# Two blocks' gate and up projections of the last feed-forward part as a two by two block product in seven products

## The chip, the cores and the metric

The kernel runs on one core of one Trainium2 chip. The metric is the device time of one execution in microseconds (us), as the median of several runs. The profile beside it is of one execution.

## The reference, cut to what matters

A two-layer decoder trunk over 256 tokens of width 1024. Each layer is a feed-forward part, a mixer and a second feed-forward part, so four feed-forward parts run in all: (layer 0, 1), (0, 2), (1, 1) and (1, 2). The change is in the last of them, (1, 2).

```python
def rms_norm(x, gain):
    y = x * rsqrt(mean(x * x, axis=-1) + 1e-6)
    return y * gain

def swiglu(h, w_gate, w_up, w_down):          # h 256x1024, w_gate and w_up 1024x2816, w_down 2816x1024
    return (silu(h @ w_gate) * (h @ w_up)) @ w_down

for layer in range(2):
    x = x + 0.5 * swiglu(rms_norm(x, ffn1_norm[layer]), ...)
    x = x + mixer(layer, x)                   # layer 0: mLSTM, layer 1: dilated attention
    x = x + 0.5 * swiglu(rms_norm(x, ffn2_norm[layer]), ...)   # layer 1: part (1, 2)
```

All arrays are float32.

## The kernel before, in words

**Three products for one.** A float32 operand is split into two parts of the type fp32r, `hi` (the rounded value) and `lo` (what is left). `mm3` then issues three matmuls for one product: `xh·wl`, `xh·wh`, `xl·wh`, each with 128 rows and up to 512 columns. Every weight therefore passes through a split: ScalarE writes `hi`, VectorE subtracts and writes `lo`.

**Tiles of a feed-forward part.** The 2816 hidden columns are 11 blocks of 256 (b = 0 to 10). For a block, the gate and the up columns stand side by side, 512 columns in all, in one PSUM bank. The 256 tokens are two halves t of 128. `gu(b, t)` is 8 steps k of 128 rows, 24 matmuls. The weights of one block are four units of two k each ([128, 1024] float32, 512 KB); each unit is used twice, by t = 0 and by t = 1. `dn(b, t)` multiplies the hidden values by the block's two units of `w_down` into PSUM accumulators: 12 matmuls for each t. Between them lies the activation: ScalarE `sil`, VectorE `h`, VectorE transposes into `hb`, which goes to DRAM (`hd`) and comes back turned (`ht`), and is split into `hhb` and `hlb` (`hidden_blocks`, `placed`).

**Order.** The matmuls' order is written out in `ffn_in`: `gu(0)`, `gu(1)`, then `gu(b)` followed by `dn(b - 2)`. `_stream` lists the weight units in the same order. A planner with a cost model (`_Model`) runs while the program is built; it places the work of ScalarE, VectorE and the queues between the matmuls by the time at which it expects operands, and so fixes the order of instructions on each engine. An engine takes its instructions in that order and waits for whichever is first.

**Rings.** `RAW` = 6 raw units may be loaded or in work. `RING` = 9 pairs of `hi` and `lo` tiles hold split units; unit n can be split when unit n - 9 has been used for the last time. Loads go out on SP's queue; no DMA is issued from POOL.

**Gains.** The norm's gain can be multiplied into x (`transposed` with a gain: four ScalarE and four VectorE instructions of 128 columns for four chunks) or into the weights (`FOLDED`: the split of one unit is then two ScalarE and two VectorE instructions of 512 columns, with a gain for each k). Part (1, 2) has its gain in the weights, and `mixer_b` ends with `then(None)`.

```python
    def loads(self):
        while self.loaded < len(self.units) and len(self.raw) + len(self.running) < RAW and \
                (self.units[self.loaded][1] is not None or self.loaded == self.next):
            self.load_unit()
```

Of the kernel before, what the change touches and what calls it, by code (L numbers as in the profile page):

```python
# [28 lines left out]

RING = 9  # L30
RAW = 6
# [19 lines left out]

FOLDED = {("kv",): 3, ("gu", 1, 1): 4, ("bq",): 5, ("gu", 1, 2): 6, ("mkv", 0): 7, ("mkv", 1): 8}

# [4 lines left out]
def folded(key):  # L58

    return next((FOLDED[key[:n]] for n in (1, 2, 3) if key[:n] in FOLDED), None)  # L60


def _stream():
# [26 lines left out]
    def ffn(layer, which):  # L90
        g, u, d = (f"ffn{which}_w_{s}" for s in ("gate", "up", "down"))

        def gu(b):
            lo, hi = b * FB, (b + 1) * FB
            proj(("gu", layer, which, b), None, layer, ((g, lo, hi), (u, lo, hi)), 2)

        def dn(b):
            for c in range(2):
                rows = "turned" if turned(layer, which, b) else None
                units.append((("dn", layer, which, b, c), (d, layer, rows, 2 * b + c, 1), D))  # L100

        gu(0)
        for b in range(1, NB - 1):
            gu(b)
            if (layer, which, b) in MEMORY:
                memory(MEMORY[layer, which, b])
            if b > 1:
                dn(b - 2)
            if b in AHEAD_OF.get((layer, which), ()):
                c = next(order)  # L110
                units.append((("pre", c), ("b_w_out", 0, None, c, 1), D))
        gu(NB - 1)
        for b in range(NB - 3, NB):
            dn(b)
# [12 lines left out]
    for b in range(2):  # L127
        single(("bq", b), "b_w_q", 0, b * 512, (b + 1) * 512, 2)
    for c in B_ORDER:
        units.append((("bo", c), None, D))  # L130
    ffn(1, 2)
    return units


def _pack(units, w):

    parts = []
    for _, src, _ in units:
        if src is None:
# [147 lines left out]
class _Engine:  # L287
# [5 lines left out]
    def __getattr__(self, method):  # L293
        call, model, name = getattr(self.engine, method), self.model, self.name

        def traced(out, *args, **kw):
# [4 lines left out]
            n = out.free_size()  # L301
            if method == "dma_start" and name != "sync":
                model.run(name, 1.0 if name == "gpsimd" else 0.1, outs, ins, 2.5)
                return
            if name == "sync":
                model.run(name, max(n * out.partition_size() * 4 / 360e3, 0.06), outs, ins, 2.0)
                return
# [50 lines left out]
class _Kernel:  # L358
    def __init__(self, tc, ctx, io, out, units):
# [3 lines left out]
        self.units = units  # L363
        self.index = {u[0]: i for i, u in enumerate(units)}
        self.offset = []
        off = 0
        for _, src, width in units:
            self.offset.append(off)
            off += P * width if src else 0
        self.tiles = {}  # L370
# [5 lines left out]
        self.raw = {}  # L376
        self.stored = {}
        self.side = []
# [122 lines left out]
    def load_unit(self):  # L501
        i, self.loaded = self.loaded, self.loaded + 1
        if self.units[i][1] is None:
            return
        width = self.units[i][2]
        raw = self.rawp.tile([P, 1024], F32, tag="raw", name=f"raw{i}")
# [4 lines left out]
        self.raw[i] = raw  # L511

    def parts(self, i):
# [4 lines left out]
    def emit_unit(self):  # L518
# [12 lines left out]
        def steps(raw):  # L531
            if key[0] == "memT" and folded(("mkv", key[1])) is None:
                raw3 = raw.rearrange("p (k t) -> p k t", k=4)
                gain = self.gains[7 + key[1]][:, 4 * key[2]:4 * key[2] + 4]
                self.nc.gpsimd.tensor_tensor(
                    raw3, raw3, gain.unsqueeze(2).to_broadcast([P, 4, 2 * P]), ALU.mult)
                yield
            gain, k, each = folded(key), src[3], width // src[4]
            if gain is None:
# [4 lines left out]
            else:  # L544
# [8 lines left out]
            self.running.remove(c)  # L553
            self.loads()
# [15 lines left out]
        c = self.spawn(steps(self.raw.pop(i)))  # L570
        self.running.append(c)
        self.step(c)
# [4 lines left out]
    def loads(self):  # L577

        while self.loaded < len(self.units) and len(self.raw) + len(self.running) < RAW and \
                (self.units[self.loaded][1] is not None or self.loaded == self.next):  # L580
            self.load_unit()

    def room(self):
        while len(self.raw) + len(self.running) >= RAW:
            self.finish(self.running[0])

    def unit_ready(self):
# [8 lines left out]
        if i not in self.raw:  # L596
            return 1e9
        at = max(model.ready(self.raw[i][:, :self.units[i][2]]),
                 model.free((id(self.ring), "hi"), RING), model.free((id(self.ring), "lo"), RING))
# [13 lines left out]
    def release(self, *key):  # L613
        i = self.index[key]
        self.used[i] += 1
        while self.freed < len(self.units) and \
                self.used[self.freed] == (1 if self.units[self.freed][0][0] in ("memT", "pre") else 2):
            self.tiles.pop(self.freed)
            self.freed += 1

    def matmul(self, out, lhsT, rhs, start, stop):
        self.pe.matmul(out, lhsT=lhsT, rhs=rhs, start=start, stop=stop)  # L624
        n = out.free_size()
# [7 lines left out]

    def mm3(self, ps, x, w, start, stop):
        (xh, xl), (wh, wl) = x, w
        self.matmul(ps, xh, wl, start, False)
        self.matmul(ps, xh, wh, False, False)
        self.matmul(ps, xl, wh, False, stop)
        self.tick()
# [207 lines left out]
    def ffn(self, layer, which, after, memory=None):  # L847
        with ExitStack() as ctx:
            self.ffn_in(layer, which, after, memory, self.pool(ctx, f"ffn{layer}{which}"))

    def ffn_in(self, layer, which, after, memory, fp):
# [4 lines left out]
        nc = self.nc  # L856
        acc, chains, hT, blocks, made = [], {}, {}, {}, {}

        def activated(ps, t, out, last=False):
# [25 lines left out]
        def hidden_blocks(b, t):  # L885
            def steps(ps):
                h = self.work.tile([P, FB], F32, tag="ta", bufs=4, name="h")
                yield from activated(ps, t, h)
                if b not in blocks:
                    blocks[b] = fp.tile([P, 4, 2, 2, 32], F32, tag="hb", bufs=1, name="hb")  # L890
                nc.vector.transpose(blocks[b][:, :, :, t, :].rearrange("p j c t -> p c j t"),
# [68 lines left out]

        for b in range(NB - 1):
            if (layer, which, b) == (0, 1, 0):
# [4 lines left out]
                continue  # L967
            if (layer, which, b) == (0, 1, 1):
# [4 lines left out]
            else:  # L973
                for t in range(2):
                    gu(b, t)
            if (layer, which, b) in MEMORY:
                memory()
            if 1 < b < NB - 1:
                for t in range(2):
                    dn(b - 2, t)  # L980
        gu(NB - 1, 0)
        dn(NB - 3, 0)
        gu(NB - 1, 1)
        dn(NB - 2, 0)
        dn(NB - 1, 0)
        for b in range(NB - 3, NB):
            dn(b, 1)
# [594 lines left out]
    def run(self, stop=None):  # L1582
# [58 lines left out]
        if stop == 2:  # L1641
            return
        with ExitStack() as ctx:
            self.shared = self.pool(ctx, "shared")
            self.ffn(0, 2, store if stop == 3 else then(None))
            if stop == 3:
                return
# [55 lines left out]
```

## Time and profile before

| | |
|---|---|
| median of 3 runs | 988.46 us (987.95 to 988.94) |
| the profiled execution's own time | 988.44 us |
| span from its first to its last instruction | 986.7 us |
| TensorE (PE) busy | 979.1 us, 99% of the span, 4679 matmuls |
| VectorE (DVE) busy | 641.8 us, 65% |
| ScalarE (ACT) busy | 569.6 us, 58% |
| granted TensorE clock | 1.000 |

The time lies 1.74 us above the span. The last feed-forward part takes the span from about 803 us to the end. A matmul's row gives its own latency (about 0.39 us for 512 columns); matmuls overlap, and their rate is read from how many start in a stretch.

### The profile page before, as it was taken

How to read it: one execution, taken by the hardware profiler on the slowest of the kernel's cores; microseconds unless marked ns; L12 is line 12 of the kernel's file. 1: busy time of each engine (PE TensorE's matmuls, PEld its weight loads, DVE VectorE, ACT ScalarE, POOL GpSimd, SP SyncE). 2: the span in 40 equal slices, each digit the busy share in tenths (PEclk: the TensorE clock that was granted, in tenths of full speed). 3: DMA queues.
4: the chain of work that ended last, by engine and by line, in shares of the span. 5: the costliest groups of instructions: out<-in, count | busy, mean ns of one | idle time of the engine just before them, and what ended most of it. 6: DMA issues, size and time to landing. Idle time of an engine off the chain costs nothing.

```text
span 986.7 us, 13121 instructions
## 1 busy us (share of the span) xinstructions
PE 979.1 (99%) x4679; PEld 813.3 (82%) x4679; DVE 641.8 (65%) x988; ACT 569.6 (58%) x914; POOL 43.1 (4%) x78
## 2 busy tenths in 40 slices
PE   9999999999999999999999999999999999999998
PEld 6887888899998888888888888888887788888887
DVE  6856656567868766575576676676566776675752
ACT  7656545478786645455476565565564585454540
POOL 0001000010010000000012000000002000000000
PEclk9999999999999999999999999999999999999999
DMA  9967777346436588878657687789537457767641
GB/s 365 329 211 273 245 229 225 107 158 202 160 129 235 190 301 265 290 269 273 219 179 252 212 304 239 250 307 325 181 106 262 187 172 245 247 206 247 206 149 43
DMA packets 84905, 221.84 MB, mean 225 GB/s; under 512 B 8108, under 2 KB 29544, under 8 KB 84840
## 3 DMA queue, kind: packets, MB, share of 16 engines
q1 hardware_dynamic: 84696, 220.97, 66.7%
q8 instruction: 36, 0.59, 0.2%
q14 instruction: 29, 0.24, 0.1%
q10 hardware_dynamic: 144, 0.04, 0.0%
HBM read 201.56 MB, written 19.42 MB: 224 GB/s over the span
## 4 chain that ended last, share of the span: by engine, by line
PE 85%; ACT 2%; DVE 2%; issue 1%; POOL 1%; ACTq 0%; DVEq 0%
PE gups L624 43%; PE acc L624 23%; PE aps L624 5%; PE oacc L624 4%; PE kvps L624 3%; PE bqps L624 2%; PE mkvps L624 1%; PE tps L631 1%; ACT L297 1%; DVE lo L297 1%; DVE s L297 1%; PE tpp L631 1%; PE po L624 1%; ACT mp L297 0%; PE ms L624 0%
## 5 line engine op out<-in xcount | busy, mean ns | idle before, releaser
L297 DVE TENSOR_TENSOR lo<-raw,hi 128x1024 fp32r<-128x1024 f32 (+3 forms) x235 | 267.9, 1161 | 75.9 <-ACT hi L297 69.9
L297 ACT CAST hi<-raw 128x1024 fp32r<-128x1024 f32 (+3 forms) x235 | 230.8, 1003 | 88.1 <-PE acc L624 37.2
L624 PE MATMUL gups<-lo,xh 128*128 128x512 f32 x704 | 273.4, 390 | 0.0
L624 PE MATMUL gups<-hi,xh 128*128 128x512 f32 x704 | 272.7, 389 | 0.1
L624 PE MATMUL gups<-hi,xl 128*128 128x512 f32 x704 | 272.7, 389 | 0.0
L297 DVE SCALAR_TENSOR_TENSOR lo<-raw,gains,hi 128x512 fp32r<-128x512 f32 x232 | 160.9, 745 | 34.5 <-ACT hi L297 31.9
L297 ACT ACTIVATE hi<-raw,gains 128x512 fp32r<-128x512 f32 x232 | 153.2, 716 | 46.3 <-PE acc L624 22.5
L624 PEld LDWEIGHTS gups<-hi,xh 128*128 128x128 f32 x704 | 132.1, 188 | 27.8 <-ACT hi L297 0.8
L624 PEld LDWEIGHTS gups<-hi,xl 128*128 128x128 f32 x704 | 132.2, 188 | 27.5
L624 PEld LDWEIGHTS gups<-lo,xh 128*128 128x128 f32 x704 | 132.2, 188 | 27.4 <-DVE lo L297 0.2
L297 ACT ACTIVATE sil<-gups,rstd 128x256 f32<-128x256 f32 x88 | 41.5, 473 | 162.1 <-PE gups L624 159.5
L297 DVE SCALAR_TENSOR_TENSOR h<-gups,rstd,sil 128x256 f32<-128x256 f32 x88 | 42.1, 480 | 127.7 <-ACT sil L297 127.7
L624 PE MATMUL acc<-lo,hhb 128*128 128x512 f32 x304 | 119.5, 393 | 0.0
L624 PE MATMUL acc<-hi,hlb 128*128 128x512 f32 x304 | 118.4, 390 | 0.0
L624 PE MATMUL acc<-hi,hhb 128*128 128x512 f32 x304 | 118.3, 389 | 0.0
L624 PEld LDWEIGHTS acc<-hi,hlb 128*128 128x128 f32 x304 | 57.1, 188 | 11.9
L624 PEld LDWEIGHTS acc<-hi,hhb 128*128 128x128 f32 x304 | 57.1, 188 | 11.4
L624 PEld LDWEIGHTS acc<-lo,hhb 128*128 128x128 f32 x304 | 57.1, 188 | 11.4
L624 PE MATMUL aps<-lo,xh 128*128 128x384 f32 (+1 forms) x144 | 49.6, 345 | 0.7 <-ACT sg L297 0.7
L624 PE MATMUL aps<-hi,xl 128*128 128x384 f32 (+1 forms) x144 | 47.5, 330 | 0.0
L624 PE MATMUL aps<-hi,xh 128*128 128x384 f32 (+1 forms) x144 | 47.4, 329 | 0.0
L297 DVE STREAM_TRANSPOSE hb<-h 128x256 f32<-128x256 f32 x76 | 33.6, 442 | 15.5 <-DMA hd<-hb 14.2
(194 smaller groups left out, 990.6 us busy)
## 6 DMA issues: line engine op xcount, KB each, us to landing
raw<-in_wts SPq DMA_DIRECT2D x310, 512.0 KB, 4.7
raw<-in_wts SPq DMA_DIRECT2D x32, 384.0 KB, 3.8
hd<-hb SPq DMA_DIRECT2D x38, 256.0 KB, 5.3
ht<-hd SPq DMA_DIRECT2D x38, 256.0 KB, 4.5
wo<-hi SPq DMA_DIRECT2D x8, 512.0 KB, 6.7
wo<-lo SPq DMA_DIRECT2D x8, 512.0 KB, 6.7
hi<-wo SPq DMA_DIRECT2D x8, 512.0 KB, 4.7
lo<-wo SPq DMA_DIRECT2D x8, 512.0 KB, 6.6
```

The lines of the kernel that those rows point to most:

```text
L297: call(out, *args, **kw)
L624: self.pe.matmul(out, lhsT=lhsT, rhs=rhs, start=start, stop=stop)
L631: self.pe.transpose(out, in_, ident)
```

## The change

The weights of blocks 5 and 6 of part (1, 2), `[1024 rows, 512 + 512 columns]`, are seen as a two by two matrix: two halves of the 1024 rows by the two blocks. x is two by two as well: two token halves by two halves of the 1024 columns. Instead of eight products of 128 tokens x 512 x 512 columns, seven are made (numbered 1 to 7 in `SEVEN`), of sums and differences of the parts of x and of the weights, and the four results are put together from the seven.

- `PLANS` gives the order of part (1, 2): `a5` is the products 2, 5, 4, 3; `b5` is 1, 6, 7; `d3` (the down projection of block 3) lies between them, `d4` after them.
- `sums` makes five of the seven left operands on VectorE and splits them, before the blocks are reached.
- Three weight slots a, b, c (two tiles of [128, 1024] each, for k = 0 and k = 2) take the place of raw units. `load_parts` fills them: four plain loads of a and b, two of c, and two adding DMAs from POOL's queue into c. After product 5's split, `remade` subtracts b from a on VectorE and then adds a part into b by an adding DMA from POOL's queue; after product 3's split VectorE adds a to b; after product 4's, VectorE subtracts a from c. Products 3 and 1, 6 and 7 are split from these remade tiles (`SLOTS`).
- Products 4, 3 and 7 go on adding in the bank of products 2, 5 and 1. Before that, a copy or sum of the bank is taken (`m2` on ScalarE, `h` and `f` on VectorE), and the four results are made on VectorE (`c21`, `c12`, `c22`, `c11`).
- Part (1, 2)'s gain moves from the weights into x: `FOLDED` loses `("gu", 1, 2)`, `mixer_b` ends with `then(6)`.
- `RING` is 8 instead of 9, in the whole kernel. The pool of the shared keys and values opens after part (0, 2). The planner counts DMAs of POOL as it counts SP's.

```diff
-RING = 9
+RING = 8
+PLANS = {(1, 2): "g0 g1 g2 d0 g3 d1 g4 d2 a5 d3 b5 d4 g7 g8 d5 d6 g9 d7"}
+SEVEN = {2: (2, 3), 5: (1, 0), 4: (3,), 3: (0,), 1: (0, 3), 6: (2, 0), 7: (1, 3)}
+EARLIER = 30
+SLOTS = {2: ("a", (0,), None), 5: ("b", (3,), None), 4: ("c", (2, 0), None),
+         3: ("b", (1,), 5), 1: ("a", (), 5), 6: ("b", (), 3), 7: ("c", (), 4)}
-FOLDED = {("kv",): 3, ("gu", 1, 1): 4, ("bq",): 5, ("gu", 1, 2): 6, ("mkv", 0): 7, ("mkv", 1): 8}
+FOLDED = {("kv",): 3, ("gu", 1, 1): 4, ("bq",): 5, ("mkv", 0): 7, ("mkv", 1): 8}
...
+    def load_parts(self, pair):
+        self.open = pair
+        for m in (4, 2, 5):
+            slot, parts, _ = SLOTS[m]
+            for k in (0, 2):
+                t = self.work.tile([P, 1024], F32, tag="mem", name="pa") if slot == "a" else \
+                    self.partp[1].tile([P, 1024], F32, tag=f"p{slot}{k}", name=f"p{slot}{k}")
+                self.slots[slot, k] = t
+                self.nc.sync.dma_start(t, self.part_of(pair + (parts[0], k)))
+                for p in parts[1:]:
+                    self.nc.gpsimd.dma_start(t, self.part_of(pair + (p, k)), accum_op=ALU.add)
...
+    def remade(self, pair, m, k):
+        nc = self.nc
+        a, b, c = (self.slots.get((n, k)) for n in "abc")
+        if m == 5:
+            nc.vector.tensor_tensor(a, a, b, ALU.subtract)
+            yield
+            nc.gpsimd.dma_start(b, self.part_of(pair + (1, k)), accum_op=ALU.add)
+        elif m == 3:
+            nc.vector.tensor_tensor(b, b, a, ALU.add)
+        elif m == 4:
+            yield from self.wait(self.made[pair, 5, k])
+            nc.vector.tensor_tensor(c, c, a, ALU.subtract)
...
+        def sums():
+            yield from self.wait(*self.normed[0], *self.normed[1])
+            yield 4.0
...
+                    nc.vector.tensor_tensor(xs[t][:, q, :], hi[:, q, :].bitcast(F32),
+                                            lo[:, q, :].bitcast(F32), ALU.add)
...
+            for m in taken:
...
+                    nc.vector.tensor_tensor(d, part[x[0]], part[x[1]], ALU.subtract)
+                    yield
+                yield from self.split(*taken[m], d)
...
+        def seventh(b, m):
+            self.finish(chains["sums"])
+            s, bank = seven.setdefault(b, {}), None
+            first = m in (2, 5, 1, 6)
+            if first:
+                bank = self.bank
+                self.bank = 1 - bank
+                s[m] = bank, self.bank_of(bank, "gu")
+            else:
+                s[m] = s[{4: 2, 3: 5, 7: 1}[m]]
+                self.finish(s[{4: "m2", 3: "h", 7: "f"}[m]])
...
+            for k in (0, 2):
+                wh, wl = self.get("st", layer, which, b, m, k)
...
+                    self.mm3(ps, (hi[:, k + j, :], lo[:, k + j, :]), (wh[:, f], wl[:, f]),
+                             first and k + j == 0, k + j == 3, not first)
...
+            def m2():
+                s["e"] = self.work.tile([P, 512], F32, tag="kn", name="e")
+                nc.scalar.copy(s["e"], ps)
+                yield
+            def h():
+                yield from self.wait(s["m2"])
+                s["g"] = self.work.tile([P, 512], F32, tag="kn", name="g")
+                nc.vector.tensor_tensor(s["g"], ps, s["e"], ALU.add)
+                yield
+            def c21():
+                yield from self.wait(s["h"])
+                nc.vector.tensor_tensor(s["e"], ps, s["g"], ALU.subtract)
+                s["p"] = True
+                yield
+                yield from hidden_blocks(b, 1)(ps)
+            def c12():
+                while "p" not in s:
+                    yield 0.1
+                nc.vector.tensor_tensor(s["g"], ps, s["g"], ALU.subtract)
+                s["q"] = True
+                yield
+                yield from hidden_blocks(b + 1, 0)(ps)
+            def f():
+                while "q" not in s:
+                    yield 0.1
+                nc.vector.tensor_tensor(s["g"], ps, s["g"], ALU.add)
+                yield
+            def c22():
+                yield from self.wait(s["f"])
+                nc.vector.tensor_tensor(s["g"], ps, s["g"], ALU.add)
+                yield FREE
+                yield from hidden_blocks(b + 1, 1)(s["g"])
+            def c11():
+                nc.vector.tensor_tensor(s["e"], ps, s["e"], ALU.add)
+                yield FREE
+                yield from hidden_blocks(b, 0)(s["e"])
...
-            self.mixer_b(store if stop == 5 else then(None))
+            self.mixer_b(store if stop == 5 else then(6))
```

## Rows read from the trace of the kernel before

**Rows 1.** The page's first part: busy us, share of the span, instructions.

```profile
PE 979.1 (99%) x4679; PEld 813.3 (82%) x4679; DVE 641.8 (65%) x988; ACT 569.6 (58%) x914; POOL 43.1 (4%) x78
```

**Rows 2.** All waits of TensorE: for whom, us in total, times, longest.

```profile
PE warm L1594 <- DVE warm L297: 1.2, 1, 1.2
PE aps L624 <- ACT sg L297: 0.7, 1, 0.7
...
PE tps L631 <- ACT mp L297: 0.3, 1, 0.3
```

**Rows 3.** The chain that ended last, from 857 us and in the tail: start, us, what.

```profile
857.83 10.88 PE gups L624 x48
868.71 5.44 PE acc L624 x24
874.15 10.88 PE gups L624 x48
885.03 5.44 PE acc L624 x24
890.47 10.88 PE gups L624 x48
...
971.18 10.93 PE acc L624 x48
```

**Rows 4.** Busy time by window of one block's 16.3 us: engines, clock, DMA share, GB/s.

```profile
852.39:868.71 16.32, 16.32 (x73) 13.51 (x73) 10.54 (x17) 8.67 (x14) 0.00 (x0) 1.00 0.69 229
```

**Rows 5.** Groups by shape, 803 to 987 us: busy, mean ns, idle before.

```profile
L297 DVE SCALAR_TENSOR_TENSOR lo<-raw,gains,hi 128x512 fp32r<-128x512 f32 x76 | 52.5, 742 | 13.1 <-ACT hi L297 13.1
L297 DVE TENSOR_TENSOR lo<-raw,hi 128x1024 fp32r<-128x1024 f32 x22 | 26.3, 1220 | 6.6 <-ACT hi L297 6.2
L297 ACT CAST hi<-raw 128x1024 fp32r<-128x1024 f32 x22 | 22.5, 1051 | 6.3 <-PE gups L624 3.3 <-PE acc L624 3.0
L297 DVE SCALAR_TENSOR_TENSOR h<-gups,rstd,sil 128x256 f32<-128x256 f32 x22 | 10.6, 480 | 36.3 <-ACT sil L297 36.3
L297 DVE STREAM_TRANSPOSE hb<-h 128x256 f32<-128x256 f32 x20 | 8.9, 444 | 5.0 <-DMA hd<-hb 4.5
L297 DVE TENSOR_TENSOR hlb<-ht,hhb 128x512 fp32r<-128x512 f32 x10 | 6.9, 688 | 1.6 <-ACT hhb L297 1.5
```

**Rows 6.** VectorE's timeline, 850 to 858 us: start, us, what, count.

```profile
851.51 2.36 DVE L297 TENSOR_TENSOR lo<-raw,hi 128x1024 fp32r<-128x1024 f32 x2 [0.26 <-ACT hi L297]
853.79 0.48 DVE L297 SCALAR_TENSOR_TENSOR h<-gups,rstd,sil 128x256 f32<-128x256 f32 x1
854.30 0.45 DVE L297 STREAM_TRANSPOSE hb<-h 128x256 f32<-128x256 f32 x1
854.67 1.37 DVE L297 SCALAR_TENSOR_TENSOR lo<-raw,gains,hi 128x512 fp32r<-128x512 f32 x2
```

**Rows 7.** VectorE's timeline: one unit in the last part, the tail's last unit.

```profile
849.11 1.41 DVE L297 SCALAR_TENSOR_TENSOR lo<-raw,gains,hi 128x512 fp32r<-128x512 f32 x2 [0.65 <-ACT hi L297]
...
966.65 1.23 DVE L297 TENSOR_TENSOR lo<-raw,hi 128x1024 fp32r<-128x1024 f32 x1 [3.01 <-ACT hi L297]
```

**Rows 8.** ScalarE and VectorE where mixer A hands over with a gain.

```profile
321.26 1.16 ACT L297 ACTIVATE xh<-tps,gains 128x128 fp32r<-128x128 f32 x4
323.52 1.15 ACT L297 ACTIVATE xh<-tps,gains 128x128 fp32r<-128x128 f32 x4 [1.10 <-PE tps L631]
```

**Rows 9.** ScalarE, where mixer B hands over without one.

```profile
803.65 0.56 ACT L297 CAST xh<-tps 128x512 fp32r<-128x512 f32 x1
804.79 0.59 ACT L297 CAST xh<-tps 128x512 fp32r<-128x512 f32 x1 [0.58 <-PE tps L631]
```

**Rows 10.** DMA issues of the whole run: KB each, us to landing.

```profile
raw<-in_wts SPq DMA_DIRECT2D x310, 512.0 KB, 4.7
...
wo<-hi SPq DMA_DIRECT2D x8, 512.0 KB, 6.7
```

More of the change, by code (lines that the diff above doesn't have):

```diff
@@ L60, in folded, with _plan @@
     return next((FOLDED[key[:n]] for n in (1, 2, 3) if key[:n] in FOLDED), None)
+def _plan(layer, which):
+    default = "g0 g1 " + " ".join(f"g{b} d{b - 2}" for b in range(2, NB - 1))
+    plan, left = [], list(range(NB - 1))
+    for what, b in ((s[0], int(s[1:])) for s in PLANS.get((layer, which), default).split()):
+        if what in "ab":
+            plan += [("st", b, m) for m in ((2, 5, 4, 3) if what == "a" else (1, 6, 7))]
+            continue
+        plan.append(({"g": "gu", "d": "dn"}[what], b))
+        if what == "d":
+            left.remove(b)
+        if what == "g" and (layer, which, b) in MEMORY:
+            plan.append(("memory",))
+        if what == "d" and b + 2 in AHEAD_OF.get((layer, which), ()):
+            plan.append(("pre",))
+    return plan, left
 def _stream():
@@ L100, in dn, with st @@
                 units.append((("dn", layer, which, b, c), (d, layer, rows, 2 * b + c, 1), D))
[L102 to L109, printed above, removed]
+        def st(b, m):
+            for k in (0, 2):
+                parts = tuple((layer, which, b, i, k) for i in SLOTS[m][1])
+                units.append((("st", layer, which, b, m, k), ("parts", layer, parts, k, 2), 1024))
+        plan, left = _plan(layer, which)
+        for step in plan:
+            if step[0] == "memory":
+                memory(MEMORY[layer, which, last])
+            elif step[0] == "pre":
                 c = next(order)
                 units.append((("pre", c), ("b_w_out", 0, None, c, 1), D))
+            else:
+                last = step[1]
+                {"gu": gu, "dn": dn, "st": st}[step[0]](*step[1:])
         gu(NB - 1)
-        for b in range(NB - 3, NB):
+        for b in left + [NB - 1]:
             dn(b)
@@ L128, in _stream, with _shared @@
         single(("bq", b), "b_w_q", 0, b * 512, (b + 1) * 512, 2)
+    rest = list(order)
     for c in B_ORDER:
-        units.append((("bo", c), None, D))
+        units.append((("bo", c), ("b_w_out", 0, None, c, 1) if c in rest else None, D))
     ffn(1, 2)
     return units
+def _shared(units):
+    parts = dict.fromkeys(p for _, src, _ in units if src and src[0] == "parts" for p in src[2])
+    return [((layer, which, b, i, k),
+             (None, layer, tuple((f"ffn{which}_w_{s}", (b + i % 2) * FB, (b + i % 2 + 1) * FB)
+                                 for s in ("gate", "up")), k + i // 2 * 4, 2), 1024)
+            for layer, which, b, i, k in parts]
 def _pack(units, w):
     parts = []
-    for _, src, _ in units:
-        if src is None:
+    for _, src, _ in units + _shared(units):
+        if src is None or src[0] == "parts":
             continue
@@ L363, in __init__ @@
         self.units = units
-        self.index = {u[0]: i for i, u in enumerate(units)}
+        stored = units + _shared(units)
+        self.index = {u[0]: i for i, u in enumerate(stored)}
         self.offset = []
         off = 0
-        for _, src, width in units:
+        for _, src, width in stored:
             self.offset.append(off)
-            off += P * width if src else 0
+            off += P * width if src and src[0] != "parts" else 0
         self.tiles = {}
@@ L505, in load_unit @@
         width = self.units[i][2]
+        if self.units[i][1][0] == "parts":
+            self.load_part(i)
+            return
         raw = self.rawp.tile([P, 1024], F32, tag="raw", name=f"raw{i}")
@@ L537, in steps @@
                 yield
+            if src[0] == "parts" and SLOTS[key[4]][2]:
+                yield from self.wait(self.made[key[1:4], SLOTS[key[4]][2], key[5]])
             gain, k, each = folded(key), src[3], width // src[4]
@@ L552, in steps @@
                                                         ALU.mult, ALU.subtract)
-            self.running.remove(c)
+            if src[0] == "parts":
+                self.made[key[1:4], key[4], key[5]] = self.spawn(self.remade(key[1:4], key[4], key[5]))
+            else:
+                self.running.remove(c)
             self.loads()
@@ L597, in unit_ready @@
             return 1e9
+        key = self.units[i][0]
+        if key[0] == "st" and SLOTS[key[4]][2]:
+            c = self.made.get((key[1:4], SLOTS[key[4]][2], key[5]))
+            if c is None or not c.done:
+                return 1e9
         at = max(model.ready(self.raw[i][:, :self.units[i][2]]),
@@ L616, in release, with matmul @@
         while self.freed < len(self.units) and \
[L617 removed]
+                self.used[self.freed] == (1 if self.units[self.freed][0][0] in ("memT", "pre", "st") else 2):
             self.tiles.pop(self.freed)
             self.freed += 1
[L623 to L624 removed]
+    def matmul(self, out, lhsT, rhs, start, stop, more=False):
+        self.pe.matmul(out, lhsT=lhsT, rhs=rhs, start=start, stop=stop, skip_group_check=more)
         n = out.free_size()
@@ L857, in ffn_in @@
         acc, chains, hT, blocks, made = [], {}, {}, {}, {}
+        pairs = "a" in PLANS.get((layer, which), "")
         def activated(ps, t, out, last=False):
@@ L963, in ffn_in @@
+        seven, gain = {}, folded(("gu", layer, which))
+        if pairs:
+            taken = {m: [fp.tile([P, 4, P], F32R, name=f"t{n}{m}") for n in ("h", "l")]
+                     for m, x in SEVEN.items() if len(x) > 1 or gain is not None}
+            chains["sums"] = self.spawn(sums())
+        plan, left = _plan(layer, which)
+        for step in plan:
+            if step == ("gu", 0) and (layer, which) == (0, 1):
                 ps = [self.acc.tile([P, 512], F32, tag="acc", name="gups") for _ in range(2)]
```

124 lines of the change are left out of this document (94 added, 30 removed).

## The prediction, made before the change was run

> **What bounds the kernel now.** I read the page's busy shares first: TensorE is busy for 979.1 of 986.7 us, VectorE for 65%, ScalarE for 58% [rows 1]. A busy share does not say whether an engine is the limit, so the waits come next: TensorE waits seven times in the whole run, for 3.9 us together, and the same view from 800 us on names none [rows 2]. The chain of waits shows the same from the other side: from gu(0) of that part to its end it is TensorE alone, 48 matmuls in 10.88 us for the gate and up products of a block, 24 in 5.44 us for a down product [rows 3]. That is 0.2267 us for a matmul of 512 columns at the full granted clock. In such a window VectorE works 10.5 and ScalarE 8.7 of 16.3 us [rows 4]. So here a matmul less is 0.2267 us less, and any other engine's work costs nothing until a matmul waits for it.
>
> **What is removed.** Blocks 5 and 6 take 96 matmuls now; seven products of 12 take 84. 12 x 0.2267 = 2.72 us [rows 3]. Everything else in the change can only take from this.
>
> **When TensorE needs what.** gu(5) starts at 874.15 now, and the order up to there is kept. With the change 874.15 to 885.03 is a5 (products 2, 5, 4, 3, at 2.72 us each), d3 ends at 890.47, b5 (1, 6, 7) at 898.63, d4 at 904.07.
>
> **RING 8.** A unit is split one slot later. One slot is 1.36 us (six matmuls) while a block is in its second half, and 4 units are held through the first. The lead is large: the last unit of gu(4) is ready at 850.5 and used at 857.83 + 3 x 1.36 = 861.9, 11.4 us ahead; the shortest lead at the end of a part is that of the last down unit, ready at 967.9, used when six matmuls of dn(9) and three of dn(10) have gone by after 971.18, so 5.3 us [rows 3, 7]. One or two slots leave 2.6 us or more. I take 0. If the cover is gone, the price is one slot, 1.4 us, for each place.
>
> **The gain in x.** Four chunks then cost ScalarE 1.16 us in place of 0.56 to 0.59 [rows 8, 9], 0.6 us more for each half of each token half, and VectorE about as much. Where the mixer of layer 0 hands over this is done already, and no wait of TensorE stands there [rows 2, 8]. For t = 1 the first matmul that needs it comes 24 matmuls after the first of gu(0), 5.4 us later, and that covers it. For t = 0 it lies among mixer B's softmax work, where TensorE has a wait of 0.3 us already [rows 2]. Bounds: 0, and 1.2 us if both halves of t = 0 go straight into such a wait. I take 0, since the split of a weight unit becomes cheaper at the same time: two instructions of 0.742 us become one of 1.220 on VectorE [rows 5].
>
> **VectorE in the dense stretch.** Before, a unit served two token halves; a unit of the seven products serves one, so 14 units are split where there were 8, at twice the pace. With eight slots, product 5's units get theirs when gu(4, 1) has used k = 0 and k = 2, at 863.27 + 1.36 = 864.6 and 866.0; product 2's are done by then. From 864.6 to the start of d4 at 898.6, 34.0 us, VectorE must do:
> - 15 splits (12 of the seven products, two of d3, the first of d4) and 6 remade tiles. No row shows a difference of two float32 tiles of 1024 columns; the nearest is the split's own, 1220 ns, and a further one in a row adds 2.36 - 1.22 = 1.14 us [rows 5, 6]. Below I take 1.05 (ScalarE's pass over 1024 columns [rows 5]), above 1.37 (two instructions of 512 columns [rows 6]). 21 x 1.14 = 23.9.
> - five sums of a PSUM bank (h, c21, c12, f, c22) and two hlb, 512 columns each, 0.69 alone and some 0.61 in a row [rows 5]: 4.3.
> - three activations, h and hb, 0.48 + 0.44, less 0.08 overlap each [rows 5, 6]: 2.3.
>
> Together 30.5 of 34.0 us, 90%. So it fits, but the lead, over 9 us before, shrinks. Laid one after the other from 865.8 (slot and ScalarE's pass), the second splits end near 880 for product 3, 884 for d3, 888.5 for product 1, 892.3 for 6, 894.5 for 7, and the first of d4 at 896.3; TensorE wants them at 883.7, 886.4, 891.8, 894.6, 897.3 and 898.6. That is 2.3 us or more each time. After that VectorE's load drops below 60% and the lead comes back. Earlier, `sums` costs 4 + 5 x 2 instructions of about 0.61, 8.5 us, in windows where VectorE is idle for 5.8 of 16.3 us [rows 4]: 0.
>
> **The new waits.** Product 4 may start only when ScalarE has copied product 2 (`m2`), product 3 when `h` is done, product 7 when `f` is done. In each case one product, 2.72 us, lies between. Behind a split (1.22) and a remade tile (1.14) and with its own 0.69, `h` takes up to 3.05 us, 0.3 too long. The copy of 0.6 us stands behind one pass of 1.05 us: covered. I take 0.2 us each for `h` and `f`, 0.4 together; bounds 0 and 0.7.
>
> **The adding DMAs.** Those into c have over 20 us. Those into b do not. Product 5's second difference a - b ends at 864.6 + 1.36 for the slot, then hi, lo and the VectorE work before it, near 871.0. From there the adding DMA of 512 KB has to land, then ScalarE and VectorE split it (1.05 + 1.22), and `h` (0.69) stands behind that split on VectorE and must end by 882.3, when product 3 starts. That leaves 8.3 us. Before has no adding DMA and none from POOL. The nearest rows are a load of 512 KB, 4.7 us, as the lower bound, and, as the upper, a store of it and then a load, 6.7 + 4.7 = 11.4 us [rows 10]. I take about 7, nearer to the load, since the fixed part comes once: covered. At 11.4 product 3 starts 3.1 us late.
>
> The Trainium skill, page "DMA: Bandwidth & Descriptors", section "Anatomy of one DMA", gives a POOL-issued transfer 2.0 us and its bytes at 436 GB/s, 3.2 us here by that figure; "Collectives: The Full Stack", section "The bandwidth ceiling", says that an adding DMA needs two source reads, which would make it an estimate of 4.4 us. The trace has 4.7 us for a plain load, so the figure is optimistic here; no run here shows the second read.
>
> **Sum.** Span 986.70 - 2.72 + 0.4 = 984.4 us; with the 1.74 us around it 986.1 us. The profiled execution, 988.44 us, stands at the median of the runs, 988.46, so no correction follows.
>
> **Rivals.**
> 1. *VectorE becomes the bound of the stretch.* For: 90% leaves 3.5 us, and its splits idle 13.1 + 6.6 us before ScalarE's half in a stretch of 184 us, 11% [rows 5], which would be 3.6 us in 34. With remade tiles at 1.37 us instead of 1.14 another 1.4. Against: part of that idle time is only ring-limited, and the leads above have to be used up first. It gives 30.5 + 3.6 + 1.4 - 34.0 = 1.5 us late, up to 2.5 with `h` and `f` worse: 987.2 to 988.2 us, 20%.
> 2. *The adding DMA is late, but not very*, 9 to 12 us: TensorE waits 0.7 to 3.7 us before product 3: 986.8 to 989.8 us, 15%.
> 3. *Slower: the adding DMA is starved.* Place: the same wait before product 3. It decides from a landing time of 8.3 + 2.3 = 10.6 us on, where the gain is gone, and the kernel is slower by over 0.2% from 12.6 us. It could be starved because SP's loads use 69% of the DMA engines' time in this stretch [rows 4] and because POOL itself has to prepare it while VectorE works 90% of the time. At 15 us it is 6.7 us of waiting: 992.8 us, 10%. For a mechanism of this kind the trace of before shows nothing either way, as POOL is idle there [rows 4]. The Trainium skill, page "SBUF — State Buffer", section "SBUF: two separate sides", states such a trap: while VectorE runs an instruction that takes both its ports, POOL can't write descriptors. It names copies and single-input operations for this, not a two-input subtraction; VectorE's groups in this part are of two inputs or a transpose, so by that rule it should not spring.
> 4. *The hand-over from mixer B or one slot less costs 0.8 to 2 us* somewhere: 987 to 988 us, 5%.
>
> **How the numbers follow.** The forecast has 50%, with its own range of 985.6 (no wait in `h` and `f`, nothing elsewhere) to 986.5. A run of this kernel tells 0.2%, 2.0 us, from no change: faster means below 986.5 us, slower above 990.4. Rivals 1, 2 and 4 fall almost wholly between. So faster 0.52, same 0.38, slower 0.10. The range for 8 in 10 begins at 985.4 us, a little below the full 2.72 us, and reaches over rivals 1, 4 and most of 2 to 988.6; above it lie rival 3 and the end of 2, some 0.13.
>
> **What would show it.** Right: TensorE's chain in a5 and b5 without gaps, 48 and 36 matmuls in 10.9 and 8.2 us; VectorE near 90% from 865 to 899 us; adding DMAs landing within 8 us; POOL busy only briefly. Wrong: a wait of TensorE named after `h` or g, or ScalarE idle before product 3's hi until the DMA has landed (rivals 2, 3); gups or acc waiting for lo, with VectorE over 95% busy (rival 1); a new wait near 786 to 805 us, or any in the earlier parts (rival 4). The prediction is wrong as a whole if the stretch is 3 us shorter and the time is not.

## The result and the profile after

The changed kernel takes 991.03 us, the median of 7 runs (990.3 to 992.8), against 988.46 us (987.72 to 988.94) before: a ratio of 1.0028, 95% interval 1.0017 to 1.004. It is slower by 2.6 us, where 986.1 us was forecast. The profiled execution took 990.69 us, with a span of 989.0 us.

The page's first part (to be held against [rows 1]):

```profile
PE 979.1 (99%) x4667; PEld 812.9 (82%) x4667; DVE 661.4 (67%) x988; ACT 568.2 (57%) x894; POOL 48.3 (5%) x82
```

Twelve matmuls are gone, and TensorE is busy just as long as before. Busy time counts matmuls that run at a lower clock, too, so this view doesn't show the reason. The chain that ended last, from gu(4) on (start, us, what), shows the place:

```profile
856.35 6.81 PE gups L751 x30
...
870.43 0.61 DVE hlb L348
871.04 0.04 issue
871.08 6.66 PE acc L751 x22
877.74 11.28 PE gups L751 x48
889.02 5.44 PE acc L751 x24
894.46 8.80 PE gups L751 x36
903.26 5.44 PE acc L751 x24
...
973.10 10.93 PE acc L751 x48
```

Before, gu(4) began at 857.83 [rows 3]; now it begins at 856.35, so the kernel comes to this place 1.48 us ahead. gu(4) would end at 856.35 + 10.88 = 867.23. The down product of block 2 should take 5.44 us and lasts until 877.74, which is 10.51: **5.07 us are lost there**. The seven products take 11.28 and 8.80 us, 0.40 and 0.64 more than 48 and 36 matmuls need. With -1.48 + 5.07 + 0.40 + 0.64 - 2.72 = +1.91 us the tail begins at 973.10 instead of 971.18 [rows 3]. The rest of the 2.3 us between the spans lies behind the last matmuls.

What is lost in that down product, in TensorE's timeline (the bracket is the idle time before, and what ended it):

```profile
868.29 0.50 PE L751 MATMUL acc<-lo,hhb 128*128 128x512 f32 x1 [1.07 <-ACT hhb L348]
868.63 0.40 PE L751 MATMUL acc<-hi,hhb 128*128 128x512 f32 x1
871.08 0.80 PE L751 MATMUL acc<-hi,hlb 128*128 128x512 f32 x1 [2.06 <-DVE hlb L348]
```

and in windows of 1 us (busy us of PE, PEld, DVE, ACT and POOL, granted clock, DMA share, GB/s):

```profile
871.00:872.00 1.00, 0.92 (x2) 0.82 (x3) 1.00 (x2) 0.00 (x0) 0.00 (x0) 0.50 1.06 209
873.00:874.00 1.00, 1.00 (x4) 0.81 (x3) 0.63 (x1) 0.00 (x0) 0.00 (x0) 0.50 1.03 205
875.00:876.00 1.00, 1.00 (x7) 0.81 (x6) 0.00 (x0) 0.00 (x0) 0.00 (x0) 1.00 1.10 380
```

TensorE waits 1.07 us for block 2's `hhb` and, two matmuls on, 2.06 us for its `hlb`. From 867.23 to 871.08 only two matmuls were started, so 3.85 - 2 x 0.2267 = 3.4 us go by. Then the granted clock is 0.50 (1.2 GHz of 2.4) from 871 to 874, and the 22 matmuls that follow take 6.66 instead of 4.99 us, another 1.7. Together that is the 5.07.

Why are block 2's hidden values late? Their way is `hb` to DRAM (`hd`), back (`ht`), ScalarE's `hhb`, VectorE's `hlb`. On SP's queue:

```profile
837.45 0.90 SPq L348 DMA_DIRECT2D pc<-in_wts  x2
838.39 1.10 SPq L348 DMA_DIRECT2D pa<-in_wts  x2
839.54 2.11 SPq L348 DMA_DIRECT2D pb<-in_wts  x2
...
843.62 0.33 SPq L348 DMA_DIRECT2D hd<-hb  x1
...
858.98 0.38 SPq L348 DMA_DIRECT2D ht<-hd  x1
```

The six plain loads of the slots go out together, 3 MB, and behind them the store of block 2's hidden values. `ht` can be issued only when `hd` has landed, 15.4 us later. The DMA view of 836 to 880 us, first by queue (q0 holds the adding DMAs; packets, MB, share of 16 engines), then by transfer (count, KB each, median us to landing):

```profile
q1 hardware_dynamic: 4176, 9.43, 58.3%
q0 software_dynamic: 576, 2.10, 26.0%
...
raw<-in_wts SPq DMA_DIRECT2D x8, 512.0 KB, 13.2
...
pc<-in_wts POOLq DMA_DIRECT2D x2, 512.0 KB, 10.9
pb<-in_wts POOLq DMA_DIRECT2D x2, 512.0 KB, 5.7
hd<-hb SPq DMA_DIRECT2D x3, 256.0 KB, 12.2
```

A raw unit that took 4.7 us to land [rows 10] takes 13.2. The adding DMAs move 2.10 of 11.53 MB, 18%, and take 26.0 of 84.3 parts of the engines' packet time, 31%. In the stretch from 852 to 858 us, in which the two adding DMAs into c run, the view by queue has:

```profile
q0 software_dynamic: 221, 0.84, 69.7%
q1 hardware_dynamic: 224, 0.79, 35.4%
```

The two queues get through as many packets as each other and nearly as many bytes, but POOL's queue takes twice the engines' time for them. SP's queue, with all other transfers on it, is left a third.

Before, block 2's `hhb` was made 18.8 us ahead of dn(2), which began at 868.71 [rows 3]:

```profile
849.90 0.62 ACT L297 CAST hhb<-ht 128x512 fp32r<-128x512 f32 x1 [0.21 <-DMA ht<-hd]
```

After, `ht` is not even issued before 858.98, so most of that lead is gone on the queue. The last part of the way is on the engines. ScalarE's and VectorE's timelines:

```profile
857.28 1.05 ACT L348 CAST hi<-raw 128x1024 fp32r<-128x1024 f32 x1 [5.86 <-DMA raw<-in_wts]
...
867.26 0.47 ACT L348 ACTIVATE sil<-gups,rstd 128x256 f32<-128x256 f32 x1 [0.30 <-PE gups L751]
867.63 0.61 ACT L348 CAST hhb<-ht 128x512 fp32r<-128x512 f32 x1
```

```profile
864.27 1.23 DVE L348 TENSOR_TENSOR lo<-pb,hi 128x1024 fp32r<-128x1024 f32 x1 [0.97 <-ACT hi L348]
...
868.81 1.22 DVE L348 TENSOR_TENSOR lo<-pc,hi 128x1024 fp32r<-128x1024 f32 x1
869.95 0.48 DVE L348 SCALAR_TENSOR_TENSOR h<-gups,rstd,sil 128x256 f32<-128x256 f32 x1
870.34 0.69 DVE L348 TENSOR_TENSOR hlb<-ht,hhb 128x512 fp32r<-128x512 f32 x1
```

ScalarE sat idle for 5.86 us until a raw unit came. `hhb` stands behind `sil` of gu(4, 1), and that can't begin before gu(4)'s last matmul; `hlb` stands behind five instructions of 1.22 us on the slots' tiles, from 864.27 on. So the values are late twice over: the transfers are slow, and the planner, which counts the slots' DMAs on SP's clock, has put their conversion late in each engine's order.

### The profile page after: what moved, and what is told of

Read it like the earlier page. It is cut to its first block, busy times and chain, and to the rows that moved or that the text cites. A ratio compares the mean times of both kernels' runs of the same rounds, so it can differ in the third digit from the quotient of the medians.

```text
span 989.0 us, 13091 instructions
## 1 busy us (share of the span) xinstructions
PE 979.1 (99%) x4667; PEld 812.9 (82%) x4667; DVE 661.4 (67%) x988; ACT 568.2 (57%) x894; POOL 48.3 (5%) x82
## 4 chain that ended last, share of the span: by engine, by line
PE 95%; DVE 2%; ACT 2%; issue 1%; POOL 0%; ACTq 0%; DVEq 0%
PE gups L751 48%; PE acc L751 24%; PE aps L751 6%; PE oacc L751 4%; PE kvps L751 3%; PE bqps L751 2%; PE mkvps L751 2%; PE tps L758 1%; ACT L348 1%; DVE s L348 1%; PE po L751 1%; PE sc L751 1%; ACT mp L348 0%; PE tpp L758 0%; PE pn L751 0%
## 5 line engine op out<-in xcount | busy, mean ns | idle before, releaser
L348 DVE TENSOR_TENSOR lo<-raw,hi 128x1024 fp32r<-128x1024 f32 (+2 forms) x271 | 312.1, 1169 | 84.6 <-ACT hi L348 76.4
L348 ACT CAST hi<-raw 128x1024 fp32r<-128x1024 f32 (+2 forms) x271 | 268.1, 1010 | 106.4 <-PE acc L751 50.5
L751 PE MATMUL gups<-lo,xh 128*128 128x512 f32 x680 | 264.4, 391 | 0.0
L751 PE MATMUL gups<-hi,xh 128*128 128x512 f32 x680 | 263.9, 390 | 0.0
L751 PE MATMUL gups<-hi,xl 128*128 128x512 f32 x680 | 263.9, 390 | 0.0
L751 PEld LDWEIGHTS gups<-hi,xl 128*128 128x128 f32 x680 | 127.9, 188 | 26.9
L751 PEld LDWEIGHTS gups<-hi,xh 128*128 128x128 f32 x680 | 127.8, 188 | 26.9 <-ACT hi L348 0.7
L348 DVE SCALAR_TENSOR_TENSOR lo<-raw,gains,hi 128x512 fp32r<-128x512 f32 x144 | 100.2, 747 | 17.9 <-ACT hi L348 16.5
L348 ACT ACTIVATE hi<-raw,gains 128x512 fp32r<-128x512 f32 x144 | 94.7, 716 | 21.8 <-PE gups L751 9.5
L348 ACT CAST hhb<-ht 128x512 fp32r<-128x512 f32 x38 | 23.5, 620 | 42.3 <-DMA ht<-hd 42.0
```

Source lines behind the costliest of these rows:

```text
L348: call(out, *args, **kw)
```

## The experiments

Theory A: the slots' loading (six loads and two adding DMAs in a burst) takes the DMA engines away from block 2's hidden values and the raw units. Theory B: the order that the planner makes of it, not the transfers, is what costs. Theory C: something else of the change (ring, gain, sums) is dear.

**1. Without the seven products.** The ring of 8, the gain in x and the pool stay. `sums` goes with the products, and `hb` has one buffer again where the products bring a second.

```diff
-PLANS = {(1, 2): "g0 g1 g2 d0 g3 d1 g4 d2 a5 d3 b5 d4 g7 g8 d5 d6 g9 d7"}
+PLANS = {}
```

> The changed kernel with the order of before in the last part: no seven products, but RING 8, the gain in x and the moved pool stay. Both theories: the earlier parts are 1.5 us ahead of before, as in the changed kernel, and the last part runs without a wait: 987.0 us. If those edits cost something in the last part, 988 us or more.

Measured: 987.22 us, ratio 0.9987 (0.9977 to 0.9996), span 985.9 us. TensorE waits nowhere in the last part; gu(4) begins at 857.08 in this profile, 0.75 us ahead of before and not the 1.5 that was expected. These edits cost nothing; they bring 1.2 us, and theory C falls for the ring and the gain. For `sums` it falls with experiment 6, whose late version has them and no wait of TensorE from 800 us to the seven products. The seven products therefore cost 991.03 - 987.22 = 3.8 us instead of bringing 2.3.

**2. Small loads in the same order.** Each load or adding DMA of the slots moves one eighth of its columns, while the planner still counts it whole; POOL clears the slots first. The hidden values of blocks 5 and 6 are thereby others than the reference's.

```diff
-                self.nc.sync.dma_start(t, self.part_of(pair + (parts[0], k)))
+                self.tc.nc.gpsimd.memset(t, 0.0)
+                self.eighth("sync", t, self.part_of(pair + (parts[0], k)))
```

> The changed kernel with the same order on every engine, but the six loads and four adding DMAs of the weight parts move an eighth of their columns (the rest of the slots is zero, so the two blocks' values are left out). Theory A (the burst of loads makes block 2's way through DRAM late on the chip, and that alone stops TensorE): its hd lands in about 5 us in place of 15, the wait before dn(2) falls under 0.5 us, the clock stays at full speed, 986 us. Rival B (the order itself: hhb and hlb of block 2 stand behind the seven products' splits on ScalarE and VectorE): the wait of about 3 us and the lower clock stay, 990.5 to 991 us.

Measured: 990.37 us, ratio 1.0015 (1.0006 to 1.0025), a little under rival B's range. The ten executions of this one program run from 988.47 us at a mean granted clock of 1.000 to 991.02 at 0.997. TensorE's waits in the last part (for whom, us, times, longest):

```profile
PE acc L756 <- DVE hlb L348: 2.1, 1, 2.1
PE acc L756 <- ACT hhb L348: 1.1, 1, 1.1
```

The waits are the same to a tenth, and on ScalarE `hhb` follows `sil` of gu(4, 1) at 867.92 without a wait for `ht`. So with this order the wait comes even when the values are there, as B says. The run is not clean: the clearing on POOL held SP's loads up, and `hd` went out only at 852.70. It doesn't show what the transfers alone would cost.

**3. The order that doesn't know of the burst.** The whole change, but the planner counts the slots' loads on a clock of their own. The program's transfers are those of the changed kernel; the order of the rest is made as if they took nobody's time.

```diff
-                self.nc.sync.dma_start(t, self.part_of(pair + (parts[0], k)))
+                self.aside("sync", t, self.part_of(pair + (parts[0], k)))
...
+        self.model.run("parts", 1024 * P * 4 / 360e3, [t], [], 2.0)
```

> The changed kernel with the same burst on the chip, but the planner does not count the slots' loads on SP's queue, so it puts hhb and hlb of block 2 where they would stand without the burst. Theory A (the data themselves come late on the chip): hd takes 12 us or more, and an engine stands waiting for ht or for a raw unit; TensorE waits 2 to 4 us, 989.5 us or more. Theory B (only the order was late): no wait before dn(2), 985.5 to 986.5 us.

Measured: 998.08 us, ratio 1.0104 (1.0086 to 1.0122). TensorE's waits in the last part, a row of the chain, and one of ScalarE's timeline:

```profile
PE gups L756 <- DVE h L348: 3.5, 2, 2.7
PE gups L756 <- DVE lo L348: 2.9, 1, 2.9
PE gups L756 <- DVE g L348: 1.9, 1, 1.9
```

```profile
842.27 15.17 DMA hd<-hb
```

```profile
861.13 0.62 ACT L348 CAST hhb<-ht 128x512 fp32r<-128x512 f32 x1 [12.51 <-DMA ht<-hd]
```

B alone falls with this. The transfers are late on the chip whatever the planner thinks: ScalarE stands for 12.51 us before `hhb`, with weight splits waiting behind it, and an order that ignores the lateness is 7 us worse. So the planner had cause to put `hhb` late. Whether it put it later than it had to is not shown: no order between the two was tried.

**4. The burst alone, in three kinds.** The kernel of experiment 1 gets the burst at the beginning of block 3, unknown to the planner and read by nobody: six loads and two adding DMAs; the six loads only; and six loads with two plain copies from POOL's queue in place of the adding DMAs.

```diff
+                    for n in range(parts):
...
+                        if n:
+                            raw.gpsimd.dma_start(t, src, accum_op=ALU.add)
+                        else:
+                            raw.sync.dma_start(t, src)
```

> The kernel without the seven products (first of this call) with a burst of the same size that nobody reads: six loads of 512 KB and two adding DMAs on top, issued where gu(3) starts, unknown to the planner, so that the order of all other work stays. Theory A: a block's hd takes over 12 us, dn(2) or dn(3) waits 2 to 4 us, the clock drops, 990 to 992 us. Rivals B and C: the lead of the ring and of the hidden values covers it, 987 to 987.5 us.

> The kernel without the seven products with the burst of six plain loads alone, no adding DMA. If the volume is what hurts (3.1 of 4.2 MB): three quarters of the burst's 6.4 us over the kernel without it, 991 to 992.5 us. If the adding DMAs' slow packets hurt: 987.2 to 989 us.

> The kernel without the seven products and with the unread burst of six loads and two DMAs from POOL's queue (993.6 us with the adding ones), where the two from POOL's queue are plain copies of the same 512 KB into the same tiles. Nobody reads the burst. Theory A1 (it is that they add): near the burst of six plain loads, 986.8 to 988.5 us. Rival A2 (1 MB more in the same stretch is enough, or that POOL issues them, adding or not): near the burst with the adding ones, 992 to 994 us. The share of each in the 6.8 us between those two runs is read from where the time falls.

Measured: with adding DMAs 993.63 us, ratio 1.0055 (1.004 to 1.007); six loads only 986.83 us, 0.9992 (0.9982 to 1.0002); with plain copies 988.58 us, 1.001 (1.0001 to 1.0019). TensorE's wait in the last part is 4.1 us for a `lo` in the first, none in the second, 1.9 us in the third. Against experiment 1's 987.22 us, the six loads cost nothing that can be measured. Plain, the further 1 MB costs 1.75 us; because it adds, another 5.05. So of the 6.8 us about a quarter is bytes and three quarters is the adding. This split is rough. One of the ten executions with six loads took 991.40 us, and three of the eleven with copies took 990.36 to 991.76, all at a mean clock of 0.998 where the others have 0.999 or 1.000. It is also a split of the time and not of the delay. Block 2's `ht` lands after 9.5 us (six loads), 13.0 (copies) and 15.1 (adding), and ScalarE stands waiting for it each time; TensorE stops only for what exceeds the lead of its operands, 0, 1.9 and 4.1 us. After the longest stop the next 36 matmuls take 10.07 us, at a lower clock, against 8.50 after the middle one. The adding burst, then the copying one: q0 in 836 to 880 us, and the window 852 to 856.

```profile
q0 software_dynamic: 288, 1.05, 12.0%
...
852.00:856.00 4.00, 4.00 (x19) 3.34 (x18) 0.00 (x0) 0.00 (x0) 0.00 (x0) 1.00 1.06 245
```

```profile
q0 software_dynamic: 288, 1.05, 5.8%
...
852.00:856.00 4.00, 4.00 (x20) 3.30 (x19) 0.00 (x0) 0.00 (x0) 0.00 (x0) 1.00 1.03 407
```

The same number of packets with the same bytes takes 12.0% instead of 5.8% of the engines' time, 2.1 times as much, and in a stretch in which the engines are full both times they move 245 instead of 407 GB/s. The Trainium skill, page "Collectives: The Full Stack", section "The bandwidth ceiling", says of the add in a reduce-scatter that it needs two source reads, which puts twice the reads on the same ring. The trace agrees with its 2.1, for a transfer into SBUF; that the second read is the reason here was not tested. The page "DMA: Bandwidth & Descriptors", section "Queues, rings and completion order", says that each DMA engine takes turns between the queues, a packet at a time. The trace fits that: 221 and 224 packets of the two queues from 852 to 858 us in the changed kernel. But one for one is not shown for every stretch: beside the adding burst here, where SP's packets are smaller, it is 148 and 287 from 852 to 856 us. In both, POOL's queue takes two thirds of the packet time, and what is on SP's queue has to wait.

**5. The burst without the adding DMAs into c.** The changed kernel with one thing undone: VectorE adds slot a to slot c, two instructions. The six loads stay in one burst, the adding DMAs into b stay.

```diff
-                for p in parts[1:]:
-                    self.nc.gpsimd.dma_start(t, self.part_of(pair + (p, k)), accum_op=ALU.add)
+                if slot == "a":
+                    self.spawn(self.plus(k))
...
+        self.nc.vector.tensor_tensor(c, c, a, ALU.add)
```

> The changed kernel with one thing undone: c's part 0 is not added by adding DMAs from POOL's queue; VectorE adds slot a to slot c in two instructions. The six plain loads of the slots stay together at the beginning of block 3, and the adding DMAs into b stay. Theory A (the burst is too much for the DMA engines because of the two adding DMAs into c): the six plain loads alone cost nothing (the run of the burst of plain loads had no wait), so block 2's hidden values come back in time, the wait before dn(2) goes, and the time is 984.5 to 986.5 us. Rival (six loads in front of the hidden values on SP's queue are enough, whatever is added): the wait of about 3 us and the clock's fall stay, 989.5 to 991.5 us.

Measured: 985.64 us, ratio 0.9973 (0.9964 to 0.9982), 5.4 us less than the changed kernel. ScalarE, and all of TensorE's waits from 800 us on:

```profile
858.45 0.62 ACT L348 CAST hhb<-ht 128x512 fp32r<-128x512 f32 x1 [0.54 <-DMA ht<-hd]
```

```profile
PE gups L757 <- DVE g L348: 0.8, 1, 0.8
PE gups L757 <- ACT e L348: 0.3, 1, 0.3
```

Block 2's `hd` lands in 9.5 us in place of 15.3, its `hhb` comes at 858.45, 9.2 us earlier, and the wait before dn(2) is gone. This settles it inside the changed kernel: the burst of six loads alone does not stop TensorE, and with the two adding DMAs in it it does. What it doesn't separate is the way: the planner, too, counts two DMAs less, and moves its order. The products' own waits are larger here than in the changed kernel: from gu(4) at 856.81 to d3 at 885.75 us, a5 takes 12.62 us in place of 10.88.

**6. The loads spread.** The changed kernel, with the slots' tiles loaded one at a time and so many units ahead of the first product; first early, then late.

```diff
-EARLIER = 30
+TURNS = (("c", 0, 24), ("c", 2, 21), ("b", 0, 18), ("b", 2, 15), ("a", 0, 11), ("a", 2, 8))
...
+TURNS = (("c", 0, 18), ("c", 2, 17), ("b", 0, 9), ("b", 2, 6), ("a", 0, 5), ("a", 2, 4))
```

> The changed kernel with the same loads, but one tile of a slot at a time, spread over blocks 0 to 4 instead of all six in 4 us. Theory A and rival B (a planner that sees the burst places hhb late): no wait before dn(2), 985 to 986.5 us. Rival C (VectorE is too full in the stretch whatever the loads do): a wait of 2 us or more remains near dn(2) or in the seven products, 988 us or more.

> The changed kernel, same order of products, adding DMAs kept; the six tiles of the slots are loaded one at a time, c with blocks 2 and 3, b and a just before a5. Theory B (the wait before a down product comes from where the load burst pushes hhb and hlb): no wait before dn(0) to dn(2), clock 1.000, 985.5 to 986.3 us. Rival C (VectorE too full in the dense stretch): waits of 2 us or more among the seven products, 988 us or more. A wait of about 1 us for h or f is expected by both.

Measured: early 987.7 us, ratio 0.9994 (0.9985 to 1.0004); late 984.92 us, 0.9963 (0.995 to 0.9976). The early one missed its expectation: the wait was not gone but had moved to block 0's hidden values, 1.1 us for `hhb` and 1.0 us for `hlb` before dn(0); why there was not followed up. Spread late, one wait of TensorE is left, 0.4 us for VectorE's tile h, and the chain leaves TensorE in one place only, from 875 to 892 us, where it runs through VectorE's work for the products:

```profile
856.39 10.88 PE gups L758 x48
867.27 5.44 PE acc L758 x24
872.71 2.73 PE gups L758 x12
...
892.17 5.74 PE gups L758 x24
897.91 5.44 PE acc L758 x24
```

The adding DMAs into c are still there. Outside the burst they do not stop TensorE, which is the other half of experiment 5. This version is faster than the kernel before by 0.4% and than the changed one by 6.1 us; against experiment 1 it gains 2.3 us.

**7. Spread, and c's sum on VectorE.** Both remedies, with gu(4) ahead of dn(1) and load times of its own.

```diff
-PLANS = {(1, 2): "g0 g1 g2 d0 g3 d1 g4 d2 a5 d3 b5 d4 g7 g8 d5 d6 g9 d7"}
+PLANS = {(1, 2): "g0 g1 g2 d0 g3 g4 d1 d2 a5 d3 b5 d4 g7 g8 d5 d6 g9 d7"}
```

> As the one before, but c's sum is made by VectorE from c and a instead of two adding DMAs, and the plan has g4 before d1 (g3 g4 d1 d2 a5). Two transfers of 512 KB less, two VectorE subtractions' worth (2.3 us) more, made before the dense stretch. Theory B: no wait before the down products, under 1 us among the products: 984.5 to 985.5 us. Rival C: VectorE's extra 2.3 us make it as slow as the one before or slower.

Measured: 985.59 us, ratio 0.997 (0.9959 to 0.9981). This is just above the expected range, and no better than the late loads alone: there the adding DMAs were already out of the way. The time is what rival C names, but no wait of TensorE is named, so VectorE's extra work is not shown as the reason.

## Why the prediction was wrong, point by point

**The step that failed** is "The adding DMAs. Those into c have over 20 us." It asked whether the transfer meets its own deadline, which it does (10.9 us to landing). It did not ask what the transfer takes from the others. The slots' plain loads had no term at all. Nobody in the prediction stood behind them on SP's queue, though block 2's `hd` and the raw units do. It took block 2's hidden values to be ready as before: its sum for VectorE from 864.6 us on has two `hlb`, and three ran there, block 2's among them. In place of 0 the runs give 5.07 us: 3.4 us before and in dn(2), 1.7 us from the clock after it. Experiment 5 and the late version of experiment 6 take the adding DMAs out of the burst in two ways, and both remove this.

**The clock** had no term either. A wait was priced at its own length; after this one the half clock added half as much again.

**The twelve matmuls**, 2.72 us, were right: from gu(4)'s start to d4's end the late version takes 903.35 - 856.39 = 46.96 us against 906.79 - 857.83 = 48.96 before ([rows 3]: gu(6) from 890.47, with 10.88 for it and 5.44 for d4). That is 2.00 less, with 0.72 of waits in the seven products (46.96 less 204 matmuls at 0.2267).

**The waits among the products**, put at 0.4 us for `h` and `f` with bounds of 0 and 0.7, were under-sized: 1.04 us in the changed kernel (a5 0.40, b5 0.64), 0.72 in the late version and 1.74 in experiment 5. They are not all of the forecast kind. The weight loads of the changed kernel wait (us, times, longest) for:

```profile
PEld gups L751 <- DVE h L348: 0.7, 2, 0.4
PEld gups L751 <- DVE g L348: 0.5, 2, 0.2
PEld gups L751 <- ACT e L348: 0.4, 1, 0.4
```

The tile g is what the chains `h` and `f` write. ScalarE's copy e had been called covered. The tile h belongs to the activation, which still reads the bank that product 1 or 6 takes next; this had no term, and it is the one wait that the late version names.

**RING 8 and the gain** were put at 0; together with the moved pool they bring 1.2 us (experiment 1). Which of them, and by what change in the order, was not tried apart. **The sums**, put at 0 too, cost TensorE nothing in the late version of experiment 6.

**VectorE** was right: 30.5 us of work in the 34.0 us from 864.6 on were forecast, 30.67 are busy in that window, though TensorE had begun a5 3.6 us late by then. That delay also gave VectorE room, so the changed kernel can't show whether rival 1 was right. Without it the chain does run through VectorE in the products, and 0.72 us (late version) to 1.74 us (experiment 5, with two more additions on VectorE) are lost there, against the 1.5 to 2.5 that rival 1 gave.

**The adding DMA into b** was forecast at 7 us and landed in 5.7, with VectorE busy for 90% of the time. Rivals 2 and 3 put the danger there, before product 3. Rival 3 named the right kind of transfer and the right sign, at the wrong place, and saw the adding DMA as the one that starves. It is the one that starves others. That rival 3's 992.8 us lies near the measured 991.03 is luck: its wait did not occur.

**Theories.** A holds as the origin: the lateness is on the chip, and experiment 4 splits it. B holds for how the lateness reaches TensorE: experiment 2 has the wait without the transfers' bytes, experiment 3 a larger loss without the planner's knowledge. How much of the 3.4 us an ideal order for the same burst would leave was not tried.

## What to carry to other kernels

Price a transfer not only by its own deadline but by what it takes from its neighbours: list all that share its stretch of the DMA engines, and count an adding DMA at twice its bytes. A store and reload that feeds TensorE suffers twice from a burst ahead of it in the queue, since its second transfer waits for its first; here a lead of 18.8 us was used up. If a planner fixes the order by its own count of the transfers, both a count that is too low (experiment 3) and a late place that follows from a high one (experiment 2) stop TensorE. Spreading the same transfers over the blocks, or moving the sum to an engine with room, turned 2.6 us lost into 2.8 to 3.5 us won here. A wait of a few microseconds can cost more than its length where the granted clock falls after it.

## What the runs showed of the hardware

- An adding DMA of 512 KB took 2.1 times the DMA engines' time of a plain copy of the same size from the same queue (12.0% against 5.8% of 44 us for two). Outside the burst it landed in 5.7 us, where a plain load took 4.7 before; in the burst it took 10.9. Why it costs twice was not tested.
- Beside adding DMAs on POOL's queue, SP's queue was left a third of the packet time: 35.4% against 69.7% from 852 to 858 us in the changed kernel, with as many packets (224 and 221).
- While two adding DMAs ran in a full stretch (experiment 4), the engines showed the same busy share (1.06 against 1.03) and moved 245 instead of 407 GB/s. The busy share doesn't show the difference; the rate does.
- After 1.07 and 2.06 us of waiting, two matmuls apart, the granted clock was 0.50 for 3 us and 22 matmuls took 6.66 instead of 4.99 us. After the same two waits in experiment 2 the 22 took 8.15 us in the profiled execution, and one of its ten executions kept a mean clock of 1.000. In the adding burst of experiment 4 a wait of 4.1 us was followed by 0.57 from 864 to 868; after the 1.9 us of the copying burst it stayed at 1.00 in the profiled execution, but three of the eleven have a mean clock of 0.998. The same program did not always get the same clock.
- Six loads of 512 KB in one burst ahead of the reload of a block's hidden values made it land in 9.5 us, where the median over the kernel before is 4.5, and cost TensorE no wait in the profiled execution (experiment 4).
